# A decoder trunk on one core: gate transposes one unit later, modulation adds freed from the gates, and two modulation steps moved into the convolution

## The chip, the cores and the metric

One core of a Trainium2 chip runs the whole program. The metric is the device time of one execution in microseconds (us); lower is better. The engines are TensorE (PE, with PEld for its weight loads), VectorE (DVE), ScalarE (ACT), GpSimd (POOL) and SyncE (SP, which issues nearly all DMAs here).

## The reference, cut to what matters

One sequence of 256 tokens with 2048 channels runs through two layers. Each layer has a token mixer (S5 in layer 0, a Conformer convolution in layer 1) and then a SwiGLU feed-forward network (FFN), each followed by a LayerNorm. The conditioning vector gives six modulation vectors per layer, one product with a 2048 x 12288 matrix each layer:

```
mod = silu(c) @ ada_w[i] + ada_b[i]          # shift, scale, gate for mixer and FFN
h = x * (1 + sc_m) + sh_m
y = s5_mixer(h) if i == 0 else conv_mixer(h)
x = layer_norm(ALPHA * x + (1 + gt_m) * y)
h = x * (1 + sc_f) + sh_f
x = layer_norm(ALPHA * x + (1 + gt_f) * swiglu_ffn(h))

conv_mixer(u): v = a * sigmoid(b)  with  a, b = split(u @ w_pw1)     # first pointwise product
               v = causal depthwise convolution, 31 taps, + b_dw
               silu(layer_norm(v)) @ w_pw2                           # second pointwise product
swiglu_ffn(u): (silu(g) * v) @ w_down  with  g, v = split(u @ w_gu)
```

The inner width of the FFN is 5632. Everything is float32.

## The kernel before, in words

**Units.** Each large product is done in float32 accuracy by splitting both factors into a high and a low part: three matmuls per product (high by high, high by low, low by high). Weights come in units of 1 MB (512 rows x 512 columns, or the like). For a unit SP issues one or two DMAs (L586) into a raw tile of a ring of four buffers (`rawp`, L517), ACT makes the high part `whi` (L860), DVE makes the low part `wlo` (L861), which frees the raw buffer, and PE runs its matmuls (L931 where the activations are the stationary side, L935 where the weights are). `whi` and `wlo` have two buffers each.

**Panels.** An FFN panel is four units and makes 256 gate and 256 value columns for all tokens. The FFN has 22 of them in two parts (12, then 10), and after each part comes the down projection of that part. After a panel the gates are formed in `ffn`: ACT takes the sigmoid (L1286), DVE multiplies twice (L1287, L1288), both for each half of the tokens. The gated tile then has to be turned: four transposes on PE (L947), and a split into high and low on ACT (L951) and DVE (L952). `turning.put(n, ...)` says how many units later that is placed; `Later` only counts units.

**Modulation steps.** A modulation vector outside the first ones is not computed by PE but by DVE, row by row: a step takes 128 rows of the 2048 columns of a full vector as one 1 MB raw tile of the same ring (`rawa`, DMA at L687) and adds it, scaled by `silu(c)`, into the tile `adaacc` (L702; the first one of a vector is L700). Sixteen steps make a full vector. Then PE sums `adaacc` over the partitions (`adar`, L710), ACT copies, PE turns it (`adat`, L718), and DVE writes `mod` (L719). `AdaQueue` orders this: `tick` is called once per unit, adds `rate` to a credit, and takes a step for each whole credit, unless `hold` is set. Taking a step issues its DMA at that place in SP's queue; its add is placed on DVE by `run`, behind given instructions (`queue_behind`). In the FFNs these are the current unit's `wlo` and what stands in `ada.after`, the last L1288 that was written.

**Order on an engine.** Each engine executes its own queue in order. The builder decides that order from the program text, estimated times and the `queue_behind` constraints, so an edit at one place can reorder rows nearby.

**The stretch of the conv mixer.** Seven panels of the first pointwise product (`gated`, `conv_in`) and two half panels (`half`) give the 16 channel chunks. Some chunks are convolved by PE, as groups of matmuls (`conv_out`, V at L1791), others by DVE, tap by tap, 31 taps a chunk (`conv_taps`, L1733, L1738, L1740). `conv_in` cuts those 31 taps into groups and spreads the groups over the units that follow: for the last one (panel 6, chunk 13) groups of nine. ACT also makes the matrices `lw` (L1650) for PE's chunks and the padded copies (L1657). `conv_end` closes the convolution (L1691 is the last gating multiply, L1715 and L1718 write the last two chunks), a LayerNorm follows, and the second pointwise product runs in three loops q = 0, 2, 3. Behind it comes FFN1, whose entry (`enter("f1", ...)`) folds the LayerNorm and the modulation vector (1, 4) into scale and bias.

Of the kernel before, what the change touches and what calls it, by code (L numbers as in the profile page):

```python
# [16 lines left out]
ADD, SUB, MUL = ALU.add, ALU.subtract, ALU.mult  # L17
# [487 lines left out]
def kernel(  # L505
# [9 lines left out]
    nc = tc.nc  # L515
# [74 lines left out]
    class Later:  # L590


        def __init__(self):
            self.now, self.todo = 0, []
# [15 lines left out]
    later, turning = Later(), Later()  # L610

    def queue_behind(instructions):

        st = ExitStack()
        for i in instructions:
            st.enter_context(tc.issue_after(i.ins))
        return st
# [28 lines left out]
    class AdaQueue:  # L646
# [5 lines left out]

        def __init__(self, parts):
            self.todo = [(l, j, b, k) for l, j, b in parts for k in range(NCH if b == 0 else NCH // 2)]
            self.credit = 0.0
            self.rate = 0.0
            self.hold = False
            self.due, self.behind, self.after = [], False, []

        def run(self, marks=()):  # L660

            due, self.due = self.due, []
            with queue_behind([*marks, *held_back, *self.after]):
                for fn in due:
                    fn()

        def tick(self):
            self.credit = min(self.credit + self.rate, 1.5)
            while self.credit >= 1.0 and not self.hold:
                self.credit -= 1.0  # L670
                self.due.append(self.step())

# [201 lines left out]
    ready, held_back, newest = [], [], None  # L874
# [66 lines left out]
    def turned(u, c0, then):  # L941

        b = aux("turned")
        for k in range(2):
            for t in range(2):
                o = k * SEQ + t * HALF
                nc.tensor.transpose(b[:, o:o + HALF], u[t][:, c0 + k * P:c0 + (k + 1) * P], ident)  # L947
        then(b.rearrange("p (k n) -> p k n", n=SEQ))

    def split(src, hi, lo):  # L950
        a = nc.scalar.copy(out=hi, in_=src)  # L951
        return a, nc.vector.tensor_tensor(out=lo, in0=src, in1=hi.bitcast(F32), op=SUB)  # L952
# [309 lines left out]
    def ffn(layer, gt, stats, wp, sp, fp, entry, ahead=None, output=None, follow=None):  # L1262

        f0, out = 0, None
        for part, nf in enumerate((24, 20)):
            f2 = fp.tile([P, 24, 2, SEQ], F32R, tag="f2", name=f"f2{layer}{part}")
            fh, fl = f2[:, :, 0], f2[:, :, 1]
            for f in range(0, nf, 2):
                if f0 + f == 0:
                    def from_entry(vs, f2=f2):  # L1270
                        for i in range(2):
                            (g, cg, _), (v, cv, t) = vs[i], vs[2 + i]
                            s = sp.tile([P, SEQ], F32, tag="h0", name="h0", bufs=1)
                            nc.vector.tensor_scalar(out=g, in0=g, scalar1=cg, scalar2=None, op0=SUB)
                            nc.scalar.activation(out=s, in_=g, func=AF.Sigmoid)
                            nc.vector.tensor_tensor(out=g, in0=g, in1=s, op=MUL)
                            nc.vector.scalar_tensor_tensor(out=v, in0=v, scalar=cv, in1=g, op0=SUB, op1=MUL)
                        split(t, f2[:, 0:2, 0], f2[:, 0:2, 1])

                    entry.panel(ffn_w_gu[layer], gu_cols(0), gu_cols(2), wp, from_entry)  # L1280
                    ada.credit = -3.0
                    continue
                acc = gemm(ffn_w_gu[layer], 0, NCH, gu_cols(f0 + f), xh, wp)
                t = sp.tile([P, 2, SEQ], F32, tag="sg", name="fsg", bufs=2)
                for i, gv in enumerate(acc):
                    nc.scalar.activation(out=t[:, i], in_=gv[:, 0], func=AF.Sigmoid)  # L1286
                    nc.vector.tensor_tensor(out=t[:, i], in0=gv[:, 0], in1=t[:, i], op=MUL)  # L1287
                    ada.after = [nc.vector.tensor_tensor(out=t[:, i], in0=gv[:, 1], in1=t[:, i], op=MUL)]  # L1288
                turning.put(2, lambda t=t, h=fh[:, f:f + 2], l=fl[:, f:f + 2]: turned([t[:, 0], t[:, 1]], 0, lambda b: split(b, h, l)))
            ada.finish(layer, 5)  # L1290
            for q in range(4):
                ada.hold = part == 1 and q >= 3
                last = part == 1 and q == 3
                if last and output:
                    output.start()
                if last and follow:
                    out = follow()
                alone = {}
                if last and output:
                    acc = [accp.tile([P, 2, SEQ], F32, tag="acc", name="acc") for _ in range(2)]  # L1300
                    alone = {"acc": acc + [aux("acc").rearrange("p (a b) -> p a b", b=SEQ)], "banks": ((0, 1), (2,), (3,)), "apart": True}
                ys = gemm(ffn_w_down[layer], f0, nf, [(512 * q, 512)], chunks(f2), wp, ahead=ahead if last else None, wide=not last, **alone)
                if alone:
                    ys = [ys[0], (ys[1][:, 0], ys[2][:, 0])]
                ada.hold = False
                if not last:
                    add_later(ys, gt, 4 * q, stats if part == 1 else None, sp)
                    continue
                for i in range(2):
                    residual(ys[i], gt, 4 * q + 2 * i, stats)  # L1310
                    if follow:
                        out.split(6 + i)
            f0 += nf
        return out
# [148 lines left out]
    with tc.manual_schedule(engines={mybir.EngineType.PE}):  # L1463
# [9 lines left out]
        for ct in range(NCH - 1):  # L1473
# [8 lines left out]
            n = plan[ct + 1]  # L1482
# [40 lines left out]
    ada = AdaQueue([(0, 3, 2), (0, 4, 0), (0, 5, 0)] + [(1, j, 0) for j in range(5)] + [(1, 5, 2)])  # L1523
# [43 lines left out]
    with mctx:  # L1567
# [41 lines left out]

        entry.split(7)  # L1610
        stats = Stats("ln01", sp)
        ada.rate, ada.behind = 0.77, True
        entry = ffn(0, mod[0][:, 5], stats, wp, sp, fp, entry, (cv_w_pw1[0], [(0, 256), (D, 256)]),
                    follow=lambda: enter("m1", stats, 0, 1, h_all, 6))
        f0ctx.close()
# [12 lines left out]
        dramp = cvctx.enter_context(tc.tile_pool(name="dram", bufs=1, space=bass.MemoryType.DRAM))  # L1628
        scr = [dramp.tile([P, 2, LP], F32, name=f"scr{i}") for i in range(8)]
        cstats = Stats("cln", sp)  # L1630
        ada.rate = 0.25
        done, taps = set(), {}

        def tap_columns(n, cs, r):
# [17 lines left out]
        def conv_in(i, t):  # L1652

            own = {0: 0, 1: 1, 2: 0, 3: 1, 5: 0}
            p, z = pad[i % 2], [pad[i % 2][:, 0], vpad[own[i]][:, 0] if i in own else pad[i % 2][:, 1]]
            for k in range(2):
                nc.scalar.copy(out=z[k][:, WIDTH - 1:LP - 1].rearrange("p (c t) -> p t c", t=2), in_=t[:, k].rearrange("p (t c) -> p t c", t=2))  # L1657
            ch = 2 * i
            mine = ch + 1 in V_CHUNKS
            vs = [cp.tile([P, 4, LS], F32, tag="vs", name="vs", bufs=3) for _ in range(1 if mine else 2)]  # L1660
            wait = {0: 5, 6: 2}.get(i, 6)

            def to_scratch():
                nc.scalar.dma_start(scr[i][:, :len(vs)], p[:, :len(vs)])

            to_scratch()
            if i == 6:
                later.put(1, lambda: conv_copies(scr[i], vs))
            else:
                later.put(wait - 2, lambda: conv_copies(scr[i], vs))  # L1670
            for k, v in enumerate(vs):
                lw, rows = taps_matrix(ch + k)
                for q, fn in enumerate(rows):
                    later.put(1 + q * (wait - 1) // 4, lambda fn=fn: behind_newest(fn))
                later.put(wait + k, lambda k=k, v=v, lw=lw: conv_out(ch + k, v, lw))
            if not mine:
                return
            acc = cp.tile([P, SEQ], F32, tag="vacc", name="vacc", bufs=2)
            begin, n = {0: (1, 7), 1: (2, 7), 2: (3, 7), 3: (4, 7), 5: (1, 8), 6: (1, 9)}[i]
            for m in range(0, WIDTH, n):  # L1680
                js = list(range(m, min(m + n, WIDTH)))
                later.put(begin + m // n, lambda js=js: behind_newest(lambda: conv_taps(ch + 1, acc, z[1], js, 0, js[-1] == WIDTH - 1)))
# [110 lines left out]
            there(ch)  # L1793

        for i in range(7):
            ada.hold = i > 5
            gated(cv_w_pw1[0], 256 * i, D, sp, lambda t, i=i: conv_in(i, t), entry if i == 0 else None, wp=wp)
        first = half(0)
        second = half(1, (cv_w_pw2[0], [(0, 1024)]))
        loads = [load_unit(ada_w[1], 4 * u, 4, [(5 * D, 512)]) for u in range(4)]  # L1800
# [87 lines left out]
        for q in (0, 2, 3):  # L1888
# [16 lines left out]
            if q == 0:  # L1905
                cvctx.close()
                fp = f1ctx.enter_context(tc.tile_pool(name="f1", bufs=1, reuse_waits="tile"))
        ada.hold = False
        stats = Stats("ln11", sp, halves=True)
        ada.rate = 0.5  # L1910
        output = Output(sp, ln_gb(1, 1)[0])
# [25 lines left out]
```

## Time and profile before

| | |
|---|---|
| median of 3 runs | 2251.38 us (2249.0 to 2252.48) |
| the profiled execution, its time | 2252.12 us |
| span from first to last instruction in its trace | 2250.3 us |
| mean granted TensorE clock | 0.996 |
| PE busy | 2200.3 us, 98% of the span |
| DVE busy | 1674.9 us, 74% |
| ACT busy | 1083.8 us, 48% |
| DMA | 578.80 MB, mean 257 GB/s |

The stages lie in the span as follows, by the trace: the entry panel of FFN0 ends at about 448 us, the first part's panels run to about 700 us and its down projection behind them, the second part's panels cover 827 to 1011 us, the conv mixer's panels some 1190 to 1350 us, the end of the convolution and its LayerNorm 1350 to 1386 us, the second pointwise product 1386 to 1515 us, and FFN1 the rest. A row of a view names the engine, the line and the tiles (out<-in). "Idle before" is the time in which the engine waited ahead of an instruction, with the instruction that ended the wait.

### The profile page before, as it was taken

What the parts mean: (1) busy time and instruction counts of PE and PEld (TensorE: products, weight loads), DVE (VectorE), ACT (ScalarE), POOL (GpSimd) and SP (SyncE); (2) the same over time, 40 slices, a digit from 0 to 9 for tenths busy, and PEclk for the clock granted to TensorE, in tenths of its full rate; (3) what the DMA queues carried; (4) which work ended last, traced back from release to release, by engine and by line L of the source; (5) the groups of instructions that cost most, each with busy time, mean ns of one, the idle gap of its engine ahead of it and who ended that gap; (6) DMA issues with size and microseconds to landing.
All of it is one profiled execution on the core that took longest, in us unless ns stands there. A gap on an engine that the chain in (4) does not pass through costs nothing. (4 is left out here: it accounts for less than half of the span.)

```text
span 2250.3 us, 33621 instructions
## 1 busy us (share of the span) xinstructions
PE 2200.3 (98%) x13555; PEld 1794.2 (80%) x13555; DVE 1674.9 (74%) x1870; ACT 1083.8 (48%) x1555; POOL 132.0 (6%) x255
## 2 busy tenths in 40 slices
PE   6999999999999999999999999999999999999998
PEld 4556778878878888888897777898888888888888
DVE  8897998878777777787979979888745444545474
ACT  4775334644343333433458775466434333434343
POOL 5761000000000000000000000000000000000000
PEclk9999999999999999999999999999999999999999
DMA  9998998589989999999856776757865555555542
GB/s 333 351 317 284 325 350 300 185 303 327 315 318 327 329 314 327 324 333 334 298 180 189 230 199 235 273 181 236 280 222 186 193 193 187 187 187 188 188 167 94
DMA packets 382306, 578.80 MB, mean 257 GB/s; under 512 B 13875, under 2 KB 281939, under 8 KB 367683
## 3 DMA queue, kind: packets, MB, share of 16 engines
q1 hardware_dynamic: 380486, 574.91, 75.1%
q8 instruction: 106, 1.74, 0.3%
q10 hardware_dynamic: 1248, 1.26, 0.2%
q0 software_dynamic: 416, 0.48, 0.1%
q14 instruction: 50, 0.41, 0.0%
HBM read 573.17 MB, written 3.42 MB: 256 GB/s over the span
## 5 line engine op out<-in xcount | busy, mean ns | idle before, releaser
L861 DVE TENSOR_TENSOR wlo<-raw,whi 128x2048 fp32r<-128x2048 f32 x343 | 785.3, 2290 | 460.8 <-ACT whi L860 459.2
L860 ACT CAST whi<-raw 128x2048 fp32r<-128x2048 f32 x343 | 653.5, 1906 | 772.3 <-PE acc L931 343.0
L931 PE MATMUL acc<-whi,h 128*128 128x512 f32 x3584 | 869.5, 392 | 7.2 <-ACT whi L860 7.0
L931 PEld LDWEIGHTS acc<-whi,h 128*128 128x128 f32 x3584 | 667.2, 188 | 155.1 <-ACT whi L860 12.1
L931 PE MATMUL acc<-wlo,h 128*128 128x512 f32 x1792 | 455.6, 391 | 3.6 <-DVE wlo L861 3.5
L931 PEld LDWEIGHTS acc<-wlo,h 128*128 128x128 f32 x1792 | 335.5, 188 | 78.5 <-DVE wlo L861 8.5
L931 PE MATMUL acc<-whi,f 128*128 128x512 f32 x1248 | 300.4, 391 | 0.0
L702 DVE SCALAR_TENSOR_TENSOR adaacc<-rawa,c_act,adaacc 128x2048 f32<-128x2048 f32 (+1 forms) x135 | 284.7, 2109 | 0.5
L931 PEld LDWEIGHTS acc<-whi,f 128*128 128x128 f32 x1248 | 232.9, 188 | 49.5 <-issue 0.8
L931 PE MATMUL acc<-wlo,f 128*128 128x512 f32 x624 | 156.5, 389 | 0.0
L931 PEld LDWEIGHTS acc<-wlo,f 128*128 128x128 f32 x624 | 117.0, 188 | 24.5
L1224 POOL CAST lnmh<-lno 128x2 fp32r<-128x2 f32 x1 | 0.2, 182 | 1945.5 <-DVE lno L68 1945.5
L935 PE MATMUL acc<-h,whi 128*128 128x256 f32 x640 | 83.8, 285 | 0.8 <-DVE h L1852 0.8
L935 PEld LDWEIGHTS acc<-h,whi 128*128 128x128 f32 x640 | 79.0, 191 | 6.5 <-issue 4.2
L1286 ACT ACTIVATE fsg<-acc 128x256 f32<-128x256 f32 x84 | 31.7, 380 | 96.8 <-PE acc L931 96.8
L630 PE MATMUL ada<-raw,c_rep 128*32 128x512 f32 (+1 forms) x576 | 69.5, 567 | 7.2 <-DMA raw<-in_ada_w_dram 7.2
L1650 ACT ACTIVATE lw<-fold,wtap 128x32 f32<-128x32 f32 x320 | 71.3, 310 | 1.4 <-PE conv L1781 1.0
L1287 DVE TENSOR_TENSOR fsg<-acc,fsg 128x256 f32<-128x256 f32 x84 | 35.1, 420 | 15.8 <-ACT fsg L1286 15.8
L935 PE MATMUL acc<-h,wlo 128*128 128x256 f32 x320 | 43.0, 283 | 0.0
L935 PE MATMUL acc<-f,whi 128*128 128x256 f32 x320 | 40.8, 284 | 0.0
L935 PEld LDWEIGHTS acc<-h,wlo 128*128 128x128 f32 x320 | 40.4, 192 | 0.0
L935 PEld LDWEIGHTS acc<-f,whi 128*128 128x128 f32 x320 | 39.4, 192 | 0.2
(368 smaller groups left out, 1831.3 us busy)
## 6 DMA issues: line engine op xcount, KB each, us to landing
raw<-in_ffn_w_gu_dram SPq DMA_DIRECT2D x352, 512.0 KB, 4.6
rawa<-in_ada_w_dram SPq DMA_DIRECT2D x128, 1024.0 KB, 5.6
raw<-in_ffn_w_down_dram SPq DMA_DIRECT2D x88, 1024.0 KB, 5.0
raw<-in_ada_w_dram SPq DMA_DIRECT2D x64, 1024.0 KB, 7.8
raw<-in_cv_w_pw_dram SPq DMA_DIRECT2D x66, 512.0 KB, 4.9
raw<-in_s_w_glu_dram SPq DMA_DIRECT2D x64, 512.0 KB, 10.2
raw<-in_cv_w_pw_dram SPq DMA_DIRECT2D x15, 1024.0 KB, 6.1
vs<-scr SPq DMA_DIRECT2D x36, 142.0 KB, 4.1
```

The costliest lines, as they stand in the source:

```text
L630: nc.tensor.matmul(acc[32 * (k % 4):32 * (k % 4) + 32, :], c_rep[:, kk, :], r[:, k, :], start=kk < 4, stop=kk >= NCH - 4)
L702: nc.vector.scalar_tensor_tensor(out=acc, in0=r[:, i], scalar=c_act[:, kk:kk + 1], in1=acc, op0=MUL, op1=ADD)
L860: m1 = nc.scalar.copy(out=hi[:, ks], in_=r[:, ks])
L861: m2 = nc.vector.tensor_tensor(out=lo[:, ks], in0=r[:, ks], in1=hi[:, ks].bitcast(F32), op=SUB)
L931: nc.tensor.matmul(acc[bank].rearrange("p a b -> p (a b)"), x[:, bank * HALF:(bank + 1) * HALF], wt[:, k], start=first, stop=end)
L935: nc.tensor.matmul(acc[bank][:, i], wt[:, k, m * P:(m + 1) * P], x, start=first and i == 0, stop=end and i == len(banks[bank]) - 1)
L1224: nc.gpsimd.tensor_copy(out=hi, in_=m)
L1286: nc.scalar.activation(out=t[:, i], in_=gv[:, 0], func=AF.Sigmoid)
L1287: nc.vector.tensor_tensor(out=t[:, i], in0=gv[:, 0], in1=t[:, i], op=MUL)
L1650: nc.scalar.mul(lw[:, q, g], fold32, wtap[:, g, 4 * c + q:4 * c + q + 1])
```

## The change

It has four edits. What follows them on the DVE and the SP queue is shown behind the diff.

1. The modulation adds no longer have to stand behind the last L1288: `ada.after` is gone.
2. The gates' transposes and splits are placed three units behind the panel, not two (both FFNs).
3. In the conv mixer the queue's rate is 0.3, not 0.25; it is held in panels 0 to 2 and open in 3 to 6 (before: open in 0 to 5), held again for the two half panels, and, from FFN0 on, it stops ahead of the vector (1, 5) until FFN1 begins. That gives four steps in the panels where there were two, and three in the second pointwise product where there were five. The vector (1, 4) is then complete two steps sooner: its `adar`, `adat` and the fold for FFN1's entry move from the loop q = 2 and the start of q = 3 to the end of q = 0.
4. The taps of the last DVE chunk in panel 6 come in groups of 11, 11 and 9 and not in 9, 9, 9 and 4.

```diff
         def run(self, marks=()):
             due, self.due = self.due, []
-            with queue_behind([*marks, *held_back, *self.after]):
+            with queue_behind([*marks, *held_back]):
                 for fn in due:
                     fn()
         def tick(self):
             self.credit = min(self.credit + self.rate, 1.5)
-            while self.credit >= 1.0 and not self.hold:
+            while self.credit >= 1.0 and not self.hold and self.todo and self.todo[0][:2] != self.until:
...
-                    ada.after = [nc.vector.tensor_tensor(out=t[:, i], in0=gv[:, 1], in1=t[:, i], op=MUL)]
-                turning.put(2, lambda t=t, h=fh[:, f:f + 2], l=fl[:, f:f + 2]: turned([t[:, 0], t[:, 1]], 0, lambda b: split(b, h, l)))
+                    nc.vector.tensor_tensor(out=t[:, i], in0=gv[:, 1], in1=t[:, i], op=MUL)
+                turning.put(3, lambda t=t, h=fh[:, f:f + 2], l=fl[:, f:f + 2]: turned([t[:, 0], t[:, 1]], 0, lambda b: split(b, h, l)))
...
-        ada.rate, ada.behind = 0.77, True
+        ada.rate, ada.behind, ada.until = 0.77, True, (1, 5)
...
-        ada.rate = 0.25
+        ada.rate = 0.3
...
-            begin, n = {0: (1, 7), 1: (2, 7), 2: (3, 7), 3: (4, 7), 5: (1, 8), 6: (1, 9)}[i]
+            begin, n = {0: (1, 7), 1: (2, 7), 2: (3, 7), 3: (4, 7), 5: (1, 8), 6: (1, 11)}[i]
...
         for i in range(7):
-            ada.hold = i > 5
+            ada.hold = i < 3
             gated(cv_w_pw1[0], 256 * i, D, sp, lambda t, i=i: conv_in(i, t), entry if i == 0 else None, wp=wp)
+        ada.hold = True
         first = half(0)
...
-        ada.hold = False
+        ada.hold, ada.until = False, None
         stats = Stats("ln11", sp, halves=True)
         ada.rate = 0.5
```

Nothing else differs; behind L1797 the changed kernel's line numbers are one higher.

**DVE at FFN0's start, before.** The rows begin in the entry panel (L1276, L1277 form its gates; L952 splits them), and the first modulation add of a vector is L700.

```order
530 L1277 SCALAR_TENSOR_TENSOR sg<-sg,ecol 128x256
531 L1276 TENSOR_TENSOR sg<-sg,h_5027 128x256
532 L1277 SCALAR_TENSOR_TENSOR sg<-sg,ecol 128x256
533 L952 TENSOR_TENSOR f_4592<-sg,f_4592 128x2x256
534 L1287 TENSOR_TENSOR fsg<-acc,fsg 128x256 x2
535 L1288 TENSOR_TENSOR fsg<-acc,fsg 128x256 x2
536 L700 TENSOR_SCALAR adaacc<-rawa,c_act 128x2048
537 L861 TENSOR_TENSOR wlo<-raw,whi 128x2048
538 L952 TENSOR_TENSOR f_4592<-turned,f_4592 128x2x256
539 L702 SCALAR_TENSOR_TENSOR adaacc<-rawa,c_act,adaacc 128x2048
```

The same place in the changed kernel:

```order
530 L1277 SCALAR_TENSOR_TENSOR sg<-sg,ecol 128x256
531 L1276 TENSOR_TENSOR sg<-sg,h_5027 128x256
532 L700 TENSOR_SCALAR adaacc<-rawa,c_act 128x2048
533 L1277 SCALAR_TENSOR_TENSOR sg<-sg,ecol 128x256
534 L952 TENSOR_TENSOR f_4592<-sg,f_4592 128x2x256
535 L1287 TENSOR_TENSOR fsg<-acc,fsg 128x256 x2
536 L1288 TENSOR_TENSOR fsg<-acc,fsg 128x256 x2
537 L861 TENSOR_TENSOR wlo<-raw,whi 128x2048
538 L702 SCALAR_TENSOR_TENSOR adaacc<-rawa,c_act,adaacc 128x2048
539 L952 TENSOR_TENSOR f_4592<-turned,f_4592 128x2x256
```

L700 moved from behind the gates to ahead of the entry panel's last L1277. In the panels that follow, the row pattern before is this one (one panel's gates, from the modulation add ahead of them):

```order
541 L702 SCALAR_TENSOR_TENSOR adaacc<-rawa,c_act,adaacc 128x2048
542 L1287 TENSOR_TENSOR fsg<-acc,fsg 128x256
543 L861 TENSOR_TENSOR wlo<-raw,whi 128x2048
544 L1288 TENSOR_TENSOR fsg<-acc,fsg 128x256
545 L1287 TENSOR_TENSOR fsg<-acc,fsg 128x256
546 L1288 TENSOR_TENSOR fsg<-acc,fsg 128x256
547 L861 TENSOR_TENSOR wlo<-raw,whi 128x2048
```

In the changed kernel the gates of that panel stand so:

```order
541 L702 SCALAR_TENSOR_TENSOR adaacc<-rawa,c_act,adaacc 128x2048
542 L861 TENSOR_TENSOR wlo<-raw,whi 128x2048
543 L1287 TENSOR_TENSOR fsg<-acc,fsg 128x256
544 L1288 TENSOR_TENSOR fsg<-acc,fsg 128x256
545 L1287 TENSOR_TENSOR fsg<-acc,fsg 128x256
546 L1288 TENSOR_TENSOR fsg<-acc,fsg 128x256
547 L861 TENSOR_TENSOR wlo<-raw,whi 128x2048
```

The first `wlo` of the next panel stands ahead of all four gate multiplies and no longer behind the first. The order of SP's DMAs in FFN0 is the same in both kernels.

**DVE in the second pointwise product, before**, behind the residual of loop q = 0: the LayerNorm sums (L765, L781, L786) and the units of q = 2.

```order
1287 L861 TENSOR_TENSOR wlo<-raw,whi 128x2048
1288 L765 TENSOR_TENSOR X<-X,shift 128x512 x3
1289 L781 TENSOR_TENSOR ln_s<-X 128x512
1290 L765 TENSOR_TENSOR X<-X,shift 128x512 x2
1291 L786 TENSOR_TENSOR ln_s<-lnsq 128x512
1292 L781 TENSOR_TENSOR ln_s<-ln_s,X 128x512
1293 L702 SCALAR_TENSOR_TENSOR adaacc<-rawa,c_act,adaacc 128x2048
1294 L786 TENSOR_TENSOR ln_s<-ln_s,lnsq 128x512
1295 L765 TENSOR_TENSOR X<-X,shift 128x512 x3
1296 L781 TENSOR_TENSOR ln_s<-ln_s,X 128x512
1297 L786 TENSOR_TENSOR ln_s<-ln_s,lnsq 128x512
1298 L861 TENSOR_TENSOR wlo<-raw,whi 128x2048 x2
```

The same place in the changed kernel, between the same `wlo` rows:

```order
1291 L861 TENSOR_TENSOR wlo<-raw,whi 128x2048
1292 L765 TENSOR_TENSOR X<-X,shift 128x512 x3
1293 L781 TENSOR_TENSOR ln_s<-X 128x512
1294 L765 TENSOR_TENSOR X<-X,shift 128x512 x2
1295 L781 TENSOR_TENSOR ln_s<-ln_s,X 128x512
1296 L786 TENSOR_TENSOR ln_s<-lnsq 128x512
1297 L765 TENSOR_TENSOR X<-X,shift 128x512 x2
1298 L786 TENSOR_TENSOR ln_s<-ln_s,lnsq 128x512
1299 L765 TENSOR_TENSOR X<-X,shift 128x512
1300 L781 TENSOR_TENSOR ln_s<-ln_s,X 128x512
1301 L786 TENSOR_TENSOR ln_s<-ln_s,lnsq 128x512
1302 L861 TENSOR_TENSOR wlo<-raw,whi 128x2048 x2
```

The modulation add between the sums is gone (and the next one, which stood behind the last row shown, too). The write of `mod` (L719) and FFN1's fold (L972 to L974), which came later, stand right ahead of the first row shown. On PE `adar` moved from q = 2 into the last unit of q = 0, and `adat` to just ahead of the LayerNorm shift (L759) at its end.

More of the change, by code (lines that the diff above doesn't have):

```diff
@@ L654, in __init__ @@
             self.todo = [(l, j, b, k) for l, j, b in parts for k in range(NCH if b == 0 else NCH // 2)]
-            self.credit = 0.0
+            self.credit, self.until = 0.0, None
             self.rate = 0.0
             self.hold = False
-            self.due, self.behind, self.after = [], False, []
+            self.due, self.behind = [], False
         def run(self, marks=()):
             due, self.due = self.due, []
-            with queue_behind([*marks, *held_back, *self.after]):
+            with queue_behind([*marks, *held_back]):
                 for fn in due:
```

## The prediction

> **What bounds the kernel now.** I read the page first: the busy times, and the chain that ended last.
>
> ```profile
> span 2250.3 us, 33621 instructions
> PE 2200.3 (98%) x13555; PEld 1794.2 (80%) x13555; DVE 1674.9 (74%) x1870; ACT 1083.8 (48%) x1555; POOL 132.0 (6%) x255
> 1564.20 21.77 PE acc L931 x96
> 1585.97 0.44 PE turned L947 x4
> ```
>
> PE is busy for 2200.3 of 2250.3 us, and the chain in the FFNs is nothing but PE: 96 matmuls in 21.77 us and four transposes in 0.44 us, 22.21 us a panel, which the change leaves alone. So it can only win or lose in the 50 us in which PE idles. Which of them lie in its stages, the waits of PE say, stage by stage: first FFN0's first part (440 to 700 us), then FFN0's second part (700 to 1160 us has this one wait), then the second pointwise product (1386 to 1515 us). FFN1, from 1515 us on, shows no wait of PE.
>
> ```profile
> PE acc L931 <- ACT whi L860: 2.7, 3, 1.2
> PE acc L931 <- DVE wlo L861: 1.0, 5, 0.2
> ...
> PE turned L947 <- DVE fsg L1288: 0.4, 1, 0.4
> ...
> PE acc L931 <- DVE wlo L861: 1.8, 1, 1.8
> ```
>
> The columns are the sum of the waits, their count and the longest. PE waits for late weights 3.7 us in FFN0's first part, 0.4 us for a gate and 1.8 us for one late `wlo`. The windows confirm the first of these (PE busy 256.25 of 260 us) and show what differs where no weights are late:
>
> ```profile
> 440.00:700.00 260.00, 256.25 (x1149) 206.85 (x1148) 201.56 (x145) 110.22 (x99) 0.00 (x0) 1.00 0.90 317
> 827.00:1011.00 184.00, 183.50 (x828) 150.26 (x828) 147.44 (x102) 72.55 (x58) 0.00 (x0) 1.00 0.94 324
> 873.00:896.00 23.00, 23.00 (x104) 18.88 (x103) 17.93 (x13) 9.15 (x8) 0.00 (x0) 1.00 0.97 338
> ```
>
> The last three columns are the granted clock, the DMA share and GB/s. The second part does the same work with PE full at 338 GB/s; so the first part's 317 GB/s is not what the queue can give but what it is asked for.
>
> **Part 1, the adds freed from the gates (FFN0).** Here is the first stall, in the rows of all engines between 446 and 460 us:
>
> ```profile
> 446.31 0.42 DVE L1276 TENSOR_TENSOR sg<-sg,h 128x256 f32<-128x256 f32 x1
> 449.88 1.28 DVE L700 TENSOR_SCALAR adaacc<-rawa,c_act 128x2048 f32<-128x2048 f32 x1
> 451.18 3.12 SPq L586 DMA_DIRECT2D raw<-in_ffn_w_gu_dram  x4
> 457.70 1.91 ACT L860 CAST whi<-raw 128x2048 fp32r<-128x2048 f32 x1 [5.60 <-DMA raw<-in_ffn_w_gu_dram]
> 459.66 0.73 PE L931 MATMUL acc<-whi,h 128*128 128x512 f32 x2 [0.27 <-ACT whi L860]
> SPq L586 <- DVE adaacc L700: 4.7, 1, 4.7
> SPq L586 <- DVE wlo L861: 82.7, 28, 4.3
> ```
>
> SP stands 4.7 us before L700 frees a raw buffer; 0.02 us after L700's end it issues the next weights, ACT casts them 6.5 us later as soon as they land, and PE waits for the cast. The change puts L700 right behind L1276, which starts at 446.31: it ends at about 446.31 + 0.42 + 1.28 = 448.0, so those weights start 3.2 us earlier.
>
> ```profile
> 457.42 1.97 PE L931 MATMUL acc<-wlo,h 128*128 128x512 f32 x8
> 451.07 2.28 DVE L861 TENSOR_TENSOR wlo<-raw,whi 128x2048 fp32r<-128x2048 f32 x1
> 486.19 0.42 DVE L1287 TENSOR_TENSOR fsg<-acc,fsg 128x256 f32<-128x256 f32 x1
> 486.53 2.28 DVE L861 TENSOR_TENSOR wlo<-raw,whi 128x2048 fp32r<-128x2048 f32 x1
> 488.88 0.92 SPq L586 DMA_DIRECT2D raw<-in_ffn_w_gu_dram  x2
> ```
>
> The 1.28 us go instead to L1277, L952, the gates and the `wlo` at 451.07; a whole L700 is their worst delay, and PE takes up that `wlo` at 457.42, 4.1 us after its end. In each later panel the first `wlo` loses the L1287 ahead of it: 486.53 becomes 486.19, and the pair that SP issues at 488.88, on that `wlo`'s end, goes 0.34 us earlier. Ten panels make 3.4 us, with the first 3.2 us a lead of 6.6 us by the end of the part. Against it stand 3.7 us of waits, plus the slow restarts: the two matmuls at 459.66 take 0.73 us where two at pace take 0.49 (8 in 1.97 us), so 0.24 us for each of five stalls (the count of the `wlo` waits), 1.2 us. That makes 4.9 us lost, and the lead covers it on paper. But the lead is not all kept: transfers that start earlier share the queue with those under way. I take **-4.0 us**, between 0 (the lead is eaten by the queue) and -4.9.
>
> ```profile
> rawa<-in_ada_w_dram SPq DMA_DIRECT2D x128, 1024.0 KB, 5.6
> raw<-in_ffn_w_gu_dram SPq DMA_DIRECT2D x352, 512.0 KB, 4.6
> ```
>
> The demand: 0.77 steps in each of four units, and the four units, 7.08 transfers of 1.049 MB in 22.21 us, are 334 GB/s; the window at 873 us gives 338. So at most 1% is left to build a lead by bandwidth, and what the edit gives is earlier starts in the gaps of the queue (a share of 0.90, not 0.97). The Trainium skill, in "DMA: Bandwidth & Descriptors", section Bandwidth, measures 341 GB/s for transfers of 1 MB and asks for 1 MB or more at a time. By that rule the lead could grow by 2% of a panel, 0.4 us; the trace's 338 GB/s agrees within 1%.
>
> **Part 2, transposes three units behind.** The transposes cost the same 0.44 us; only their place moves, by a unit of 5.5 us (21.77 / 4).
>
> ```profile
> 906.44 0.55 PE L947 MATMUL turned<-ident,fsg 128*128 128x128 f32 x3 [0.41 <-DVE fsg L1288]
> ```
>
> This one wait goes: **-0.5 us** with its restart. The gates now end later by part of an add (2.3 us) at worst, which 5.5 us cover. The gate tile has two buffers and panels are four units apart, so three units still fit; the last panel's split is needed only at the end of the down projection's rows.
>
> **Part 3, two steps more in the convolution.** Each is an add and a 1 MB DMA in SP's queue, ahead of weights and of the `vs` copies.
>
> ```profile
> L702 DVE SCALAR_TENSOR_TENSOR adaacc<-rawa,c_act,adaacc 128x2048 f32<-128x2048 f32 x2 | 4.7, 2346 | 0.0
> 1266.00:1292.00 26.00, 26.00 (x166) 20.28 (x165) 22.38 (x34) 19.30 (x58) 0.00 (x0) 1.00 0.72 224
> 1292.00:1318.00 26.00, 26.00 (x166) 20.24 (x165) 21.91 (x31) 22.15 (x62) 0.00 (x0) 1.00 0.85 228
> 1343.26 0.41 DVE L1733 TENSOR_SCALAR vacc<-pad,taps,vec 128x256 f32<-128x256 f32 x1 [4.94 <-ACT pad L1657]
> 1347.96 0.43 DVE L1691 TENSOR_TENSOR pad<-acc,sg 128x256 f32<-128x256 f32 x1 [1.11 <-PE acc L935]
> 1349.05 1.80 ACT whi L860
> 1353.16 0.40 DVE V L1740
> ```
>
> DVE idles 3.6 and 4.1 us in the two windows and then 4.94 us before L1733, 12.7 us in all; two adds of 2.35 us fit, and PE is full (26.00 of 26) throughout, with the DMA share at 0.72 to 0.85. That is the cover. If it is gone, the end pays: from 1349 us the chain goes ACT, DVE's `wlo`, the taps, to PE. The last step (now ahead of the taps at 1323 us) pushes DVE by 2.35 us, of which its idle rests before the wait take most; ACT's LayerNorm square behind it, and so the cast at 1349.05, I put 0.45 us late (a fifth of an add; bounds 0 and 1.4, if half of the rest is not covered).
>
> **Part 4, groups of 11.** Two taps move into the 1.11 us before L1691, so that two taps of 0.40 us (the last row above) leave the chain that ends the convolution: -0.8 us. With part 3, **-0.3 us**, between -0.8 and +0.6.
>
> **Part 5, two steps fewer in the second pointwise product.**
>
> ```profile
> 1445.92 2.35 DVE L702 SCALAR_TENSOR_TENSOR adaacc<-rawa,c_act,adaacc 128x2048 f32<-128x2048 f32 x1
> 1451.80 4.49 DVE L861 TENSOR_TENSOR wlo<-raw,whi 128x2048 fp32r<-128x2048 f32 x2
> 1454.14 3.16 PE L931 MATMUL acc<-wlo,h 128*128 128x512 f32 x8 [1.80 <-DVE wlo L861]
> 1463.33 0.99 PE adar L710 x8
> 1465.24 0.45 PE adat L718 x4
> ```
>
> The add at 1445.92 stands between the LayerNorm sums and the `wlo` that PE waits 1.80 us for. It goes (2.35 us), while the four small rows of the fold come ahead: with 16 columns each they lie below L1733's 0.41 us for 256 columns, 1.6 us in all at most, and I take 0.7. PE does `adar` and `adat` before this place, 1.44 us, so it needs the `wlo` that much later. 2.35 - 0.7 + 1.44 = 3.1 us against 1.8: the wait goes, with 1.3 us to spare (0.4 at the bound). **-1.9 us** with the restart; 0 if ACT's new rows hold the sums up by 3 us.
>
> **The sum:** -4.0 - 0.5 - 0.3 - 1.9 = -6.7 us. The profiled execution took 2252.12 us, 0.74 above the median of the runs; from it 2245.4, from the median 2251.38 - 6.7 = **2244.7 us**. A measurement of this kernel can tell about 0.2%, 4.5 us, from no change.
>
> **Rivals.** *B, the queue keeps what part 1 gives.* The weights that start early only wait in the queue for those under way: demand 334 against 338 GB/s speaks for it, the share of 0.90 and the 4.7 us of SP's wait against it. Then -0.5 - 0.3 - 1.9 = -2.7: 2248.7 us, no change that could be told. *C, slower: the added steps starve the ring in the convolution.* Each takes one of four raw buffers for 5.6 us of transfer and 2.35 us of add, 8.0 us, where weights now come in time. A whole unit held back so, two times, with none of it covered by the lead, is 16 us, and with the 6.7 us gained elsewhere 2260.7 us; it decides against the change only from 6.7 + 4.5 = 11.2 us lost, a lead under (16 - 11.2) / 2 = 2.4 us. The tightest unit there has a lead of 1311.71 - 1308.54 - 1.89 = 1.28 us:
>
> ```profile
> 1308.54 1.89 ACT L860 CAST whi<-raw 128x2048 fp32r<-128x2048 f32 x1
> 1311.71 0.48 PE L931 MATMUL acc<-whi,h 128*128 128x512 f32 x1
> ```
>
> That speaks for it; against it, PE has no wait at all in these windows, and the DMA share of 0.72 leaves the queue free time to catch up. *D, ACT's rows take the place of DVE's:* the added steps make ACT's LayerNorm squares and casts late at the convolution's end (part 3 at its worst, +0.6), and ACT's fold holds up the sums in the second pointwise product, so that its wait stays. Then -4.0 - 0.5 + 0.6 = -3.9, 2247.5 us, within 0.2%; for it, the cast at 1349.05 lies on the chain already; against it, the 1.3 us to spare. That the edits are not carried out is excluded by the order of the rows.
>
> **Chances.** The forecast 0.60, of which 0.04 falls within 0.2% (above 2246.9), B 0.24, of which 0.02 reaches below it, C 0.08, D 0.08. So faster 0.56 + 0.02 = 0.58, same 0.04 + 0.22 + 0.08 = 0.34, slower 0.08. The range: the best of all terms is -4.9 - 0.5 - 0.8 - 1.9 = -8.1, 2243.3, and the runs of before scatter from -2.4 to +1.1, so 2241.5 below. Above it takes in B and D and the upper scatter, 2251.0; C is left out.
>
> **What would show it.** Right: PE's waits from 440 to 700 us under 1 us; SP's issue at 451 us before 448.5, and a DMA share there of about 0.92; no wait at L947; PE's `wlo` wait near 1454 us gone; PE restarting behind the LayerNorm of the convolution with 0 to 0.8 us less behind the last cast. Wrong: late weights in the same panels with the first issue early (B), waits of PE for L860 or L861 between 1266 and 1344 us (C), a new wait in 1440 to 1460 us or L1657 later than 1344 us (D), or any wait in FFN1.

## The result

The changed kernel takes 2245.77 us in the median of 22 runs (2241.43 to 2254.62), the kernel before 2250.98 us on the same chips (22 runs, 2246.62 to 2257.13). The medians are 5.2 us apart. The ratio is 0.9979, with a 95% interval from 0.9970 to 0.9987: 4.7 us faster, between 2.9 and 6.8. The forecast was 6.7 us less, 2244.7 us.

The profiled execution of the changed kernel took 2251.7 us, one of the slowest of its 22, so its span says nothing of the gain. Its stages do. First the changed kernel's page and PE's waits in the same three windows as before (440 to 700 us, 700 to 1160 us, where nothing is listed any more, and 1386 to 1515 us):

```profile
span 2249.9 us, 33607 instructions
PE 2204.0 (98%) x13555; PEld 1799.1 (80%) x13555; DVE 1672.3 (74%) x1870; ACT 1084.3 (48%) x1555; POOL 133.2 (6%) x255
PE acc L931 <- ACT whi L860: 5.9, 5, 1.7
PE acc L931 <- DVE wlo L861: 0.8, 4, 0.2
...
PE acc L935 <- DVE h L1853: 0.8, 1, 0.8
PE lnrep L829 <- DVE lny L76: 0.2, 1, 0.2
```

The wait for a gate (L947) and the 1.8 us for the `wlo` are gone. The late weights in FFN0's first part, which were to go, are 6.7 us, where before showed 3.7. The 0.8 us for `h` (L1853) is not new: before has the same wait just ahead of 1386 us, at L1852. The windows of FFN0's two parts agree: PE is busy 253.30 of 260 us in the first (before 256.25), and all of the second.

```profile
440.00:700.00 260.00, 253.30 (x1134) 204.46 (x1134) 201.88 (x149) 107.85 (x98) 0.00 (x0) 1.00 0.89 311
827.00:1011.00 184.00, 184.00 (x833) 151.45 (x833) 143.55 (x102) 72.45 (x58) 0.00 (x0) 1.00 0.94 324
```

The end of the convolution has a new, short wait for the cast and a shorter one for the chunk at L1715 (0.7 us before):

```profile
PE acc L935 <- ACT whi L860: 0.4, 1, 0.4
PE lnsum L811 <- DVE V L1715: 0.4, 1, 0.4
```

Stages can be compared between executions although each starts a little differently: PE runs the same 344 weight units in the same order in every kernel here, so the time from the first matmul of one unit to that of another is a stage's length. Four stages matter: FFN0's first part (units 38 to 84), its second part with the way into its down projection (108 to 152), the convolution's end (192 to 196) and the second pointwise product (196 to 209). The lengths in us, for all profiles but those of the four runs that change the rate of the modulation steps (e5, e6, e9 and e10, given below):

| kernel (run) | 38 to 84 | 108 to 152 | 192 to 196 | 196 to 209 | time against before |
|---|---|---|---|---|---|
| before | 265.57 | 250.51 | 49.80 | 85.90 | |
| before again (e7) | 265.64 | 249.88 | 49.82 | 84.28 | |
| changed | 268.44 | 249.33 | 49.64 | 82.11 | 0.9979 (0.9970 to 0.9987) |
| changed again (e4) | 264.15 | 250.40 | 49.61 | 82.12 | 0.9974 (0.9963 to 0.9985) |
| changed, adds behind the gates (e1) | 261.88 | 249.97 | 49.61 | 82.12 | 0.9975 (0.9965 to 0.9985) |
| before, adds freed (e2) | 267.71 | 250.78 | 49.81 | 84.24 | 1.0006 (0.9996 to 1.0015) |
| before, steps moved (e3) | 263.44 | 251.81 | 50.37 | 82.10 | 0.9989 (0.9979 to 0.9998) |
| before, taps by 11 (e8) | 264.90 | 251.70 | 49.07 | 84.26 | |
| before, transposes three behind (e11) | 264.12 | 249.33 | 49.82 | 84.30 | 0.9991 (0.9979 to 1.0003) |

### The profile page after: what moved, and what is told of

The parts are those of the page before. It is cut to its first block, busy times and chain, and to the rows that moved or that the text cites. A ratio compares the mean times of both kernels' runs of the same rounds, so it can differ in the third digit from the quotient of the medians.

```text
span 2249.9 us, 33607 instructions
## 1 busy us (share of the span) xinstructions
PE 2204.0 (98%) x13555; PEld 1799.1 (80%) x13555; DVE 1672.3 (74%) x1870; ACT 1084.3 (48%) x1555; POOL 133.2 (6%) x255
## 4 chain that ended last, share of the span: by engine, by line
PE 80%; DVE 9%; DMA 5%; ACT 3%; issue 2%; SPq 0%; POOL 0%; POOLq 0%; DVEq 0%; ACTq 0%
PE acc L931 65%; PE acc L935 7%; DMA raw<-in_ffn_w_gu_dram 4%; DVE wlo L861 2%; PE acc L1043 2%; ACT whi L860 2%; PE turned L947 1%; PE conv L1781 1%; DVE adaacc L702 1%; PE y L499 1%; PE ada L630 1%; DMA raw<-in_s_w_glu_dram 1%; DVE pin L476 1%; DMA raw<-in_ada_w_dram 1%; PE adar L710 0%
## 5 line engine op out<-in xcount | busy, mean ns | idle before, releaser
L702 DVE SCALAR_TENSOR_TENSOR adaacc<-rawa,c_act,adaacc 128x2048 f32<-128x2048 f32 (+1 forms) x135 | 284.7, 2109 | 0.4
L951 ACT CAST f<-turned 128x512 fp32r<-128x512 f32 x42 | 24.7, 588 | 59.7 <-PE turned L947 59.7
```

Of the source, the lines that this page charges most:

```text
L702: nc.vector.scalar_tensor_tensor(out=acc, in0=r[:, i], scalar=c_act[:, kk:kk + 1], in1=acc, op0=MUL, op1=ADD)
```

## The experiments

**e1 and e2: the freed adds, taken out and alone.** e1 puts the `ada.after` lines back into the changed kernel; e2 is before without them. The edit shown is e1's; e2's is its reverse, made on before.

```diff
-            with queue_behind([*marks, *held_back]):
+            with queue_behind([*marks, *held_back, *self.after]):
...
-                    nc.vector.tensor_tensor(out=t[:, i], in0=gv[:, 1], in1=t[:, i], op=MUL)
+                    ada.after = [nc.vector.tensor_tensor(out=t[:, i], in0=gv[:, 1], in1=t[:, i], op=MUL)]
```

Expected of e1: 

> The changed kernel, but the modulation adds still stand behind the last gating multiply (part 1 undone). Theory 1, as predicted: part 1 is worth 4.0 us, so this is 2.7 us under before and its first part of FFN0 shows 3 to 5 us of waits for late weights. Theory 2, from the two traces: part 1 gives nothing, and the gain is the second pointwise product (its stall of 2.0 us and the eight matmuls at 0.43 us behind it, 3.6 us together) and the gates: then this is 4 to 5 us under before, like the changed kernel.

Expected of e2: 

> Before with part 1 alone: adds not held behind the gates, transposes two units behind. Theory 1: 4.0 us under before, and waits of PE from 440 to 700 us under 1 us. Theory 2: within 1 us of before or slower, with 3 to 7 us of waits there as in the changed kernel's trace, and new waits of PE for L1288, since a gate can now end an add (2.3 us) later.

e1: 2245.94 us, ratio 0.9975 (0.9965 to 0.9985), as fast as the changed kernel; from 440 to 700 us it waits 1.3 us for weights, where theory 1 had 3 to 5. e2: 2253.14 us, 1.0006 (0.9996 to 1.0015). In e2 PE's waits from 440 to 700 us are these:

```profile
PE turned L947 <- DVE fsg L1288: 3.0, 3, 2.0
PE acc L931 <- ACT whi L860: 1.5, 2, 1.1
PE acc L931 <- DVE wlo L861: 0.4, 2, 0.2
```

The gates now come after a `wlo` and an add, and transposes two units behind wait for them, up to 2.0 us. Theory 1 falls: freeing the adds saves no time that can be seen, with or without the other edits. What it does is lengthen the waits for the gates (3.6 us in e2's FFN0, 0.3 to 1.7 us in the kernels that hold the adds and keep two units), and three units take these away.

**e3: the moved steps alone.** The lines with `until`, 0.3, `i < 3` and the hold, on before.

> Before with the moved steps alone (rate 0.3, held in panels 0 to 2, stop ahead of the vector (1, 5)). Theory 1: 1.9 us under before less up to 0.6 us at the convolution's end. Theory 2: 3 to 4 us under before, since the stall near 1454 us and the half clock behind it both go; the windows there show a granted clock of 1.00 where before shows 0.62.

2248.74 us, 0.9989 (0.9979 to 0.9998), 2.5 us less. That interval (0.5 to 4.7 us) holds both theories; the stages decide. The second pointwise product takes 82.10 us, as in the changed kernel; the stall is gone, and the granted clock from 1450 to 1462 us is 1.00. Against e7, e8, e11 and e2 that stage is 2.2 us shorter, near theory 1; the 3 to 4 us of theory 2 hold only against an execution like before's first profile (3.8 us), in which the clock was lower behind the stall. The convolution's end takes 50.37 us, 0.57 longer than before.

**e4: the changed kernel again.**

> The changed kernel once more, for a second profile of it. Theory 1: its first profile fell on an unlucky execution, and this one shows waits of PE from 440 to 700 us under 1 us. Theory 2: 3 to 7 us again. Both: no wait near 1454 us and none at L947.

2245.37 us, 0.9974 (0.9963 to 0.9985). This execution is the better one to read, since it starts FFN0 0.4 us off before's. It waits 3.2 us for weights from 440 to 700 us, where theory 1 had less than 1. Its rows at FFN0's start, to be read against those of the prediction's first stall:

```profile
446.28 1.28 DVE L700 TENSOR_SCALAR adaacc<-rawa,c_act 128x2048 f32<-128x2048 f32 x1
447.59 7.08 SPq L586 DMA_DIRECT2D raw<-in_ffn_w_gu_dram  x4
454.61 1.91 ACT L860 CAST whi<-raw 128x2048 fp32r<-128x2048 f32 x1 [0.44 <-DMA raw<-in_ffn_w_gu_dram]
459.28 1.91 ACT L860 CAST whi<-raw 128x2048 fp32r<-128x2048 f32 x1 [2.76 <-DMA raw<-in_ffn_w_gu_dram]
466.01 1.91 ACT L860 CAST whi<-raw 128x2048 fp32r<-128x2048 f32 x1 [1.14 <-DMA raw<-in_ffn_w_gu_dram]
```

The same casts in before's trace, the first of which the prediction showed at 457.70:

```profile
457.70 1.91 ACT L860 CAST whi<-raw 128x2048 fp32r<-128x2048 f32 x1 [5.60 <-DMA raw<-in_ffn_w_gu_dram]
460.65 1.91 ACT L860 CAST whi<-raw 128x2048 fp32r<-128x2048 f32 x1 [1.04 <-DMA raw<-in_ffn_w_gu_dram]
467.21 1.91 ACT L860 CAST whi<-raw 128x2048 fp32r<-128x2048 f32 x1 [0.89 <-DMA raw<-in_ffn_w_gu_dram]
```

SP's issue came at 447.59 us (448.0 forecast, 451.18 before), the first cast 3.1 us earlier than before, and that panel lost nothing (22.23 us, before 23.32). But the next two casts are only 1.4 and 1.2 us earlier. The rows of SP that issue their weights tell why, first before's, then e4's:

```profile
453.38 0.92 SPq L586 DMA_DIRECT2D raw<-in_ffn_w_gu_dram  x2
461.96 0.92 SPq L586 DMA_DIRECT2D raw<-in_ffn_w_gu_dram  x2
453.32 1.36 SPq L586 DMA_DIRECT2D raw<-in_ffn_w_gu_dram  x2
458.87 0.92 SPq L586 DMA_DIRECT2D raw<-in_ffn_w_gu_dram  x2
```

The second pair is issued at the same time in both. Its buffer comes free with a `wlo` that ends at 453.29 us (before 453.35), and freeing the adds leaves that `wlo` where it was. The third pair is issued 3.1 us earlier, but needs 7.1 us from its issue to its cast, and not 5.3. Two panels on the lead is gone: PE waits again.

```profile
PE acc L931 <- ACT whi L860: 2.0, 2, 1.2
PE acc L931 <- DVE wlo L861: 0.2, 1, 0.2
```

That is e4 from 480 to 515 us; the panel there (units 48 to 52) takes 25.39 us, and 24.29 in before's first profile, 26.05 in its second (e7). The lead was not kept.

**e5 and e6: less demand on the ring in FFN0's first part.** Same number of steps, spread otherwise; e5 on e1's kernel, e6 on the changed one.

```diff
+            if layer == 0 and part == 0:
+                ada.rate = 0.70
             f2 = fp.tile([P, 24, 2, SEQ], F32R, tag="f2", name=f"f2{layer}{part}")
...
+            if layer == 0:
+                ada.rate = 0.85
             ada.finish(layer, 5)
             for q in range(4):
```

Expected of e5: 

> The kernel of e1 (adds behind the gates), with 0.70 modulation steps per unit in the first part's panels of FFN0 and 0.85 from its down projection on, in place of 0.77. If the waits of FFN0's first part come of the demand on the ring (7.08 transfers a panel, 334 GB/s), 6.80 a panel, 321 GB/s, remove them: units 38 to 84 take 260 to 261 us (e1 261.9, before 265.6), and new waits of up to 3 us may show in the second part, which then asks for 7.4 a panel. If they come of where the adds stand, they stay at 1 to 4 us.

Expected of e6: 

> The changed kernel (adds free of the gates) with the same split of the rate. Demand theory: units 38 to 84 take 260 to 262 us, where the changed kernel's two profiles took 268.4 and 264.2. Order theory: they stay at 264 or more, 2 us or more over e5.

One number in these expectations and in the prediction is off: since `tick` caps the credit at 1.5, a rate of 0.77 gives 3 steps in 4 units, not 3.08 (the traces have 30 `rawa` transfers in units 40 to 80). So before's demand is 7.0 transfers a panel, 330 GB/s; 0.70 gives 2 in 3 units, 6.7 a panel (315 GB/s), and 0.85 4 in 5, 7.2 a panel (340 GB/s).

e6: 2253.03 us, 1.0013 (1.0002 to 1.0024). In its first part PE is never idle, and units 38 to 84 take 257.1 us, where the order theory had 264 or more. From 700 to 1190 us it waits for the weights:

```profile
440.00:700.00 260.00, 260.00 (x1174) 214.45 (x1173) 203.28 (x149) 112.15 (x105) 0.00 (x0) 1.00 0.89 313
PE acc L931 <- ACT whi L860: 9.2, 12, 1.5
PE acc L931 <- DVE wlo L861: 1.3, 4, 0.4
```

e5: 2259.83 us, 1.0040 (1.0026 to 1.0053). Waits for weights in its first part are 1.0 us, and one of 3.4 us for an add (adar behind L702, about 589 us), which no other profile of the FFN shows; the panel that holds it takes 28.88 us, 5.0 more than in e6, of the wait and of the lower clock behind it (0.60 from 589 to 593 us). So its 264.89 us for units 38 to 84 prove nothing by themselves. Behind 700 us it waits 7.6 us for weights:

```profile
PE acc L931 <- ACT whi L860: 6.6, 13, 1.2
PE acc L931 <- DVE wlo L861: 1.0, 4, 0.4
```

At 315 GB/s asked there are hardly any late weights (none and 1.0 us), at 330 1 to 7 us in the first part, at 340 7.6 and 10.5 us behind 700 us, whether the adds stand behind the gates or not. The demand theory holds; that e5 stays at 264.89 was not foreseen by either. What the demand consists of stays open: a step that is moved away takes its transfer and its add of 2.35 us on DVE with it, and another rate also shifts the places of the steps that remain. These runs do not separate the three.

**e7 and e8: before once more, and the taps alone.** e8's edit is `6: (1, 11)`.

Expected of e7: 

> The kernel before once more, for a second profile. The stage times that vary by themselves: units 38 to 84 within 262 to 269 us. The stall near 1454 us comes again at 1.8 to 2.0 us, and the half clock behind it (1.6 us) or not, as in the run with the freed adds alone: so units 204 to 209 take 33.9 or 32.3 us.

Expected of e8: 

> Before with the taps in groups of 11 alone. The end of the convolution (units 192 to 196) takes 49.0 us, 0.8 us less than before's 49.80. With the moved steps it was 50.37 in e3 and 49.61 with both in e1, so 50.37 - 0.76. Nothing else moves.

One execution each: 2250.04 and 2252.17 us. The stages came out so, except that e8's others moved as they do between executions. e8's end of the convolution takes 49.07 us, 0.75 less than e7's 49.82. The stall near 1454 us is in both. First the window behind the stall in before's first profile, then the row of the stall in e7:

```profile
1454.00:1458.50 4.50, 4.36 (x12) 3.44 (x13) 4.50 (x4) 1.90 (x1) 0.00 (x0) 0.62 0.75 227
```

```profile
1453.65 2.14 PE L931 MATMUL acc<-wlo,h 128*128 128x512 f32 x8 [1.80 <-DVE wlo L861]
```

The window has a granted clock of 0.62 (the column behind POOL), and the prediction's row at 1454.14 shows the eight matmuls of that execution in 3.16 us; in e7 they take 2.14. The wait is 1.80 us in both.

**e9 and e10: the demand lowered in all of FFN0**, by ten steps more in the S5 mixer's panels; e9 on the changed kernel, e10 with the adds behind the gates.

```diff
-            self.credit = min(self.credit + self.rate, 1.5)
+            self.credit = min(self.credit + self.rate, 1.5 if self.rate < 1.05 else 2.5)
...
-            ada.rate = 1.05
+            ada.rate = 1.42
...
-        ada.rate, ada.behind, ada.until = 0.77, True, (1, 5)
+        ada.rate, ada.behind, ada.until = 0.70, True, (1, 5)
```

Expected of e9: 

> The changed kernel with ten of FFN0's modulation steps moved ahead into the S5 mixer's panels (34 steps there, not 24; the cap on the credit is 2.5 there), and 0.70 steps a unit in all of FFN0. Demand theory: no waits of PE for late weights in either part of FFN0 (units 38 to 84: 257 to 258 us; 108 to 152: 249 us), 7 to 11 us under the changed kernel's two profiles, less what ten adds and 10 MB cost in the S5 mixer (0 to 8 us, units 0 to 38 now 231.3). Order theory (the gates' place decides): units 38 to 84 stay at 264 to 268 us.

Expected of e10: 

> The same with the adds behind the gates, as in e1. Demand theory: within 2 us of e9. Order theory: 3 to 5 us faster or slower than e9.

e9: 2263.61 us, 1.0054 (1.0038 to 1.0071); e10: 2265.44 us, 1.0060 (1.0043 to 1.0077), 1.8 us apart. FFN0 is as the demand theory has it: units 38 to 84 take 258.8 and 259.7 us, 108 to 152 249.3 in both, and PE waits 0.2 us at most for weights from 440 us on. The S5 mixer pays far more than the 0 to 8 us allowed for it: units 0 to 38 take 255.1 us in e9, 231.6 in the changed kernel. PE's waits there (200 to 440 us), in e9 and then in e10:

```profile
PE acc L931 <- ACT whi L860: 16.1, 8, 3.8
PE adar L710 <- DVE adaacc L702: 1.8, 2, 0.9
PE acc L931 <- DVE wlo L861: 1.5, 4, 0.6
```

```profile
PE acc L931 <- ACT whi L860: 17.1, 8, 3.4
PE turned L947 <- DVE sg L1134: 0.8, 1, 0.8
```

No version that beats the changed kernel came of this: FFN0 gains 5 to 10 us and the S5 mixer loses 23.5.

**e11: the transposes three units behind, alone.**

> Before with the transposes three units behind alone. Predicted: 0.5 us under before, no wait at L947. From the profiles of before and of the runs with two units behind (0.3 to 1.7 us of waits at L947): 0.3 to 1.7 us under. A larger gain, over 2 us, would have to come from the order of DVE at FFN0's start, where this kernel may lose the first stall too.

2249.20 us, 0.9991 (0.9979 to 1.0003), so 2.0 us less with an interval that includes no change. The part with the waits at L947 (108 to 152) takes 249.33 us, and no wait at L947 is left in the FFN. The four profiles of kernels with a distance of two and the adds behind the gates (before, e7, e8, e3) have 0.4, 0.3, 1.7 and 1.6 us of them.

## Why the prediction was right or wrong

**The number** was near (2244.7 forecast, 2245.77 measured, 4.7 us faster and not 6.7), and faster was the side it gave most weight to. **Its largest term was wrong**, so the nearness is luck in part. Of its signs of being right, SP's early issue came, the wait at L947 and the `wlo` wait near 1454 us went; but PE's waits from 440 to 700 us are 6.7 us in the changed kernel and 3.2 in e4, not under 1. The ends of its range do not follow from the parts it names: 2243.3 - 2.4 is 2240.9 and not 2241.5, and B's 2248.7 + 1.1 is 2249.8 and not 2251.0. By the steps:

1. *What bounds the kernel.* Right: PE is the bound, and the gain came only where it idled. The inference that the queue can give 338 GB/s because one window of the second part shows it, so that 317 is only what is asked, was the weak link. e5, e6, e9 and e10 show how the late weights depend on the demand: none or few at 315 GB/s, microseconds at 330, 7.6 to 10.5 us at 340. So at 330 the ring of raw buffers works near the edge of what this kernel sustains. Why the second part gets through at 330 is not shown; PE waits there as well once more is asked (e5, e6).
2. *Part 1, -4.0 us.* The first step of it is shown by e4: the add moved, SP's issue and the first cast came 3.1 us earlier. The step that failed is the sum "with the first 3.2 us a lead of 6.6 us by the end of the part". The first 3.2 us are not handed on: the second pair is issued when it was before (453.32 and 453.38 us), because another `wlo` frees its buffer, and the third, issued 3.1 us earlier, takes 1.9 us longer to its cast. So the casts are 3.1, then 1.4, then 1.2 us earlier (0.4 us of each is e4's earlier start), and the lead shrinks where the sum lets it grow. The gain of 0.34 us a panel was not traced by itself. The saving is nil by time: e1 against the changed kernel, 0.9975 against 0.9979 and 0.9974, and e2 alone, 1.0006. This is rival B, to which the prediction gave 0.24. It names the longer transfers rightly, but not the second pair's unmoved issue; its time, 2248.7 us, was too high since other terms were larger. How much a given execution loses in the first part is then a matter of how its transfers fall: in e1 the pair behind the same L700 lands 5.2 us after its issue and not 6.5 (first pair below), its panel loses nothing, and the add stands behind the gates.

```profile
453.44 3.12 SPq L586 DMA_DIRECT2D raw<-in_ffn_w_gu_dram  x4
458.64 1.91 ACT L860 CAST whi<-raw 128x2048 fp32r<-128x2048 f32 x1 [1.84 <-DMA raw<-in_ffn_w_gu_dram]
```

   The table's first column shows the spread: 261.9 to 265.6 us for six profiles with the adds behind the gates, 264.2 to 268.4 for three with the adds freed (of e2's 267.7, 3.0 us are waits for gates). Whether freeing them costs 2 us there is open: the times of e1 and e4 don't show it.
3. *Part 2, -0.5 us.* Right in kind, too small: units 108 to 152 take 250.9 us in the mean of the five profiles with a distance of two (before, e7, e8, e2, e3), 249.8 in the four with three (changed, e4, e1, e11). That is 1.2 us, late weights among them (the waits at L947 alone are 0.9 us in the mean of the five); before's single wait of 0.41 us was at the low end of what a distance of two shows. e2 shows that the edit is also needed once the adds are free.
4. *Parts 3 and 4, -0.3 us.* Right: 49.61 against 49.80 to 49.82, -0.2 us, made of +0.57 for the steps (e3) and -0.75 for the taps (e8), where 0.45 and 0.8 were forecast. The cast at the end is late by the 0.4 us that the changed kernel's waits show. Rival C, a starved ring, did not come: PE has no wait between 1266 and 1344 us.
5. *Part 5, -1.9 us.* The mechanism was right: the `wlo` comes in time with both adds gone. Against e7, e8, e11 and e2 (84.24 to 84.30 us) it is -2.2 us; against before's first profile, from which the sum was made, -3.8. The difference, 1.6 us, is the lower clock behind the stall, which the prediction saw as a matmul row of 3.16 us for eight and left out of the price.

With the terms as measured: part 1 0, part 2 -1.2, parts 3 and 4 -0.2, part 5 -2.2 to -3.8, so -3.6 to -5.2 us, which holds the measured -4.7. A wrong main term and three right ones of which two were too small made a number that looks right; the stages, not the total, tell it.

## What to carry to other kernels

Before a wait for weights is put down to the one instruction that released the buffer late, change the demand: here two kinds of waits for weights were a place in DVE's order (gone with two adds) and a ring near its limit (which no order tried here took away). A lead in a buffer ring is handed on only as far as the other buffers come free earlier too and their transfers take no longer for it: look at the issue and the landing of the next two or three transfers before adding leads up. And where a single execution scatters by more than the gain, compare stage by stage over several profiles; two of these four edits could not have been sized by the total time.

## What the runs showed of the hardware

The same 1.80 us wait of PE near 1454 us, in the five profiles that have it (before, e7, e8, e11, e2), was followed once by slow matmuls (up to 0.43 us from one start to the next, not 0.23; granted clock 0.62 over 4.5 us) and four times not. The same happened in FFN0 in other runs, behind waits of 1.9 us (e7, at 507 us) and 2.1 us (e8, at 508 us). This is e7's, with eight matmuls in 2.77 us and the window's clock of 0.66:

```profile
506.96 2.77 PE L931 MATMUL acc<-whi,h 128*128 128x512 f32 x8 [1.92 <-ACT whi L860]
507.00:512.00 5.00, 5.00 (x15) 3.88 (x16) 4.61 (x3) 2.29 (x2) 0.00 (x0) 0.66 0.67 246
```

The two windows with 0.62 and 0.66 come out if the clock is at half for 3.4 us each time ((1 - 0.62) x 4.5 x 2 and (1 - 0.66) x 5 x 2, an estimate). In all thirteen profiles, from 440 to 2235 us, every such stretch stands behind a wait of 1.8 us or more (also e2's of 2.0 us at a gate and e5's of 3.4 us), and the only waits of that length without one are four of the five of 1.80 us. So by the stage's length the 1.80 us wait cost 2.2 us or 3.8; what decides which was not tested. The Trainium skill, "TensorE: Matmul & The Clock Gate", section Part 1: The HAM clock gate, puts the return to half rate after an idle window of about 3.4 us that runs free of the program; the free-running window agrees with the one time in five, but here waits of 1.9 to 2.1 us were enough. The waits of 1.2 us or less in before's and e4's FFN0, and of up to 1.7 us in the changed kernel's, were not followed by a lower clock (1.00 from 440 to 700 us in all three profiles).
